# One written order for VectorE and ScalarE from the first product on, and what stands where in it

## The chip, the cores and the metric

The kernel runs on one core of one Trainium2 chip, in one launch. The metric is the device time of that launch in microseconds (us). Engines are named as in the profile: PE is TensorE (matmuls), PEld its weight load, DVE is VectorE, ACT is ScalarE, POOL is GpSimd, SP is SyncE, which here only issues DMAs.

## The reference, cut to what matters

One transformer block on 512 tokens of width 1024, in float32. `x` is normalised and multiplied by one wide matrix; the product is split into the inputs of two branches and of their gates.

```python
n = rmsnorm(h, g_mix[l])
proj = n @ w_in[l]
(gq, gk, gv, gr, z_gf, z_gb, cq, ckv, kr, z_ma, z_mb) = jnp.split(proj, SPLIT_IDX, axis=-1)
y_gla = gla_branch(...)   # 4 heads of gated linear attention, both directions
y_mla = mla_branch(...)   # 8 heads of latent attention with rotary positions
merged = jax.nn.sigmoid(z_ma) * y_gla + jax.nn.sigmoid(z_mb) * y_mla
h = h + merged @ w_out[l]
m = rmsnorm(h, g_mlp[l])
h = h + jnp.square(jax.nn.relu(m @ w_ff1[l])) @ w_ff2[l]
return rmsnorm(h, g_final)
```

In the gated linear attention each head has decays: `log_sigmoid(z @ w_gate + b) / 16`, summed up along the tokens, and their exponentials scale `q` and `k`. `gv` and `gr` are 1024 wide each, `gq` and `gk` 128 wide for each of 4 heads, `z_mb` 1024 wide.

## The kernel before, in words

**Split products.** Every float32 operand of a matmul is split into a rounded high part and a low remainder, and each product is three matmuls (`mm3`: high by high, high by low, low by high). The split is one ACT instruction (the high part, a copy) and one DVE instruction (the remainder, a subtraction), lines 93 and 94. So before PE can use a weight, ACT and then DVE must have worked on it. Split weights live in `halves`: four buffers of high and four of low parts, used in turn. A new split has to wait until PE has finished with the buffer it gets.

**The stages.** The first product (`first`, lines 315 to 351) multiplies the normalised input by the weights of `gq` and `gk` of head 0 and of two pieces of `z_mb`. Beside it runs the sum of squares of `x` (`xss`), whose root is spread over partitions (`xdg`, `xrs`, `R`). Then come, on PE: `zb2` and `zb3` (two more pieces of `z_mb`, 24 matmuls each), the seven products of `gr`, the seven products of `gv`, with single products put in between (the "fillers"), and then the four heads (`bd`, `sc`, `gla0o` and so on), the latent attention, the output product `wo` and the feed-forward part `f`, `gx`, `gz`. The change touches what lies between the first product and the first head.

**The seven products.** `gr` and `gv` are each computed as a product of 2 x 2 blocks by seven block products instead of eight (class `Seven`), in the order 1, 2, 5, 6, 3, 7, 4. Each has 24 matmuls of 128 x 512. Sums and differences of the left blocks are made by POOL (`x_sums`: `xy`, `xz`) and split by ACT and DVE (`xsy`, `xsz`; in the changed kernel `xs`). Differences of the right blocks are made by DVE in place (`less`, line 598: tiles `grw`, `gvw`). `prepare(m)` makes the difference, if there is one, and the split of the weights of product m (`gr50h`, `gr50l`, `gr51h`, `gr51l` for product 5: two pieces, high and low); `product(m)` issues its matmuls and what reads the result. Products 1, 6, 7 and 4 add up in one pair of PSUM banks (`grx`, `gvx`), 5 and 3 in a second (`grz`, `gvz`), 2 in a third (`grw`, `gvw` as outputs of PE). After 1, 5 and 6 ACT copies the partial result out (line 645: `gra`, `grc`, `grb`); after 2, 3 and 7 DVE adds the bank to such a copy (line 650), and a "sink" follows: a tanh and a multiplication for `gr` (lines 658 and 659), a split for `gv` (lines 97 and 98). As 4 goes on in the banks of 7, its first matmuls must wait until DVE has read them after 7.

**The fillers.** `zb4` is put behind product 2 of `gr`, the small product `zk` (gate inputs and rotary key, 16 matmuls, weights `wz`) behind product 7 of `gr`, `gq1` behind product 2 of `gv`. `gk1` stands between 7 and 4 of `gv`. From `zk` come `z4` and then the gates of head 0: `gatef`, `gateb` (one matmul each), then `l` (abs, exp, a table load, ln, a table load), scans `rrf`, `rrb`, differences `diff`, `difb`, exponentials `eef`, `eeb`, small ones `e3f`, `e3b` (`gates_begin`, `gates_end`).

**What sets the order.** A scheduler orders the instructions of each engine, except where the kernel pins them: `in_program_order(start, engines)` makes the instructions issued since `start` follow each other as written. Before the change DVE and ACT are pinned in the first product (all engines, from `fixed`) and again from `heads_from` on, which stands just ahead of the gates of head 0; in between, a chain of `goes_behind` only keeps the DVE work of one `prepare` behind that of the one before. PE is pinned from `ordered` on throughout.

## Time and profile before

| what | us |
|---|---|
| median of 3 runs | 785.69 (785.46 to 786.38) |
| the profiled execution, its own time | 784.01 |
| its span, first to last instruction | 782.3 |
| PE busy in the span | 763.6 |
| DVE, ACT, POOL busy | 571.2, 443.8, 113.4 |
| mean granted clock of PE | 0.994 of full speed |

The profile is of one execution. Its span leaves out 1.7 us of that execution's own time, and that time lies 1.7 us below the median of the three runs. Views used are the page (busy times, 40 slices), the chain of waits of an engine, the timeline of an engine (start, duration, the instruction's line and operands; in square brackets the idle time ahead of it and what ended that), and windows (busy time of each engine in a stretch, with PE's granted clock, called PEclk).

### The profile page before, as it was taken

To read this page: it belongs to the slowest core of one execution; us is meant where nothing else is said; L and a number is where in the kernel's file an instruction comes from. 1 tells how busy PE (TensorE), PEld (TensorE's weight loads), DVE (VectorE), ACT (ScalarE), POOL (GpSimd) and SP (SyncE) were. 2 spreads that over 40 slices of the span, in tenths; PEclk is the share of its full clock that TensorE was granted. 3 is DMA by queue.
4 is the path that set the end of the run, shared out by engine and by line. 5 is a ranking of instruction groups with operands and counts; after the bars stand their busy time and mean duration, and the time that the engine had idled before them with its cause. 6 is when DMAs were issued, how large, how long until landed. Compare 5 with 4: busy or idle time off the path is not lost.

```text
span 782.3 us, 10154 instructions
## 1 busy us (share of the span) xinstructions
PE 763.6 (98%) x3768; PEld 642.4 (82%) x3768; DVE 571.2 (73%) x850; ACT 443.8 (57%) x749; POOL 113.4 (14%) x190
## 2 busy tenths in 40 slices
PE   9989999799999999999999999999999999999996
PEld 7768878598888888888888898888888888888885
DVE  7788896666656867699973578874787578848695
ACT  7564657364747556688853366435553455436644
POOL 0710001314426004211120000000000000000014
PEclk9999999899999999999999999999999999999999
DMA  9806110112123524222033731155106511560002
GB/s 324 282 28 181 41 28 27 41 52 72 54 54 82 121 38 103 76 82 68 28 119 97 268 110 54 52 181 145 40 16 202 147 46 35 162 182 8 27 1 107
DMA packets 93185, 73.94 MB, mean 95 GB/s; under 512 B 15088, under 2 KB 74480, under 8 KB 93136
## 3 DMA queue, kind: packets, MB, share of 16 engines
q1 hardware_dynamic: 92048, 70.14, 30.4%
q10 hardware_dynamic: 864, 2.38, 0.9%
q0 software_dynamic: 224, 0.79, 0.3%
q8 instruction: 29, 0.48, 0.3%
q14 instruction: 20, 0.16, 0.1%
HBM read 69.62 MB, written 2.10 MB: 92 GB/s over the span
## 4 chain that ended last, share of the span: by engine, by line
PE 89%; DVE 6%; ACT 2%; issue 1%; DMA 1%; POOL 0%; SPq 0%; POOLq 0%; DVEq 0%
PE f L89 8%; PE f L88 7%; PE f L90 7%; PE gx L88 4%; PE gx L89 4%; PE gx L90 4%; PE first L323 2%; PE za L88 2%; PE za L89 2%; PE wo L90 2%; PE wo L89 2%; PE gz L89 2%; PE za L90 2%; PE gz L88 2%; PE gz L90 2%; PE wo L88 2%
## 5 line engine op out<-in xcount | busy, mean ns | idle before, releaser
L1395 POOL DMA_DIRECT2D gfin<-in_g_final x1 | 0.7, 653 | 282.6 <-PE f L90 282.6
L1220 DVE TENSOR_TENSOR w<-w,w 128x1024 f32<-128x1024 f32 x32 | 38.8, 1223 | 0.4
L892 DVE TENSOR_REDUCE top<-s 128x1 f32<-128x512 f32 x32 | 21.8, 681 | 5.2 <-PE s L90 5.1
L895 ACT ACTIVATE e<-s,top 128x512 f32<-128x512 f32 x32 | 21.9, 687 | 5.6 <-DVE top L892 3.0
L457 POOL COPY v3f<-rrf 128x4 f32<-128x4 f32 x4 | 2.8, 710 | 148.6 <-DVE rrf L446 148.6
L1167 DVE TENSOR_TENSOR h<-gx,h 128x512 f32<-128x512 f32 x32 | 21.6, 687 | 1.8 <-PE gx L90 1.8
L94 DVE TENSOR_TENSOR pT<-tp,pT 128x512 fp32r<-128x512 f32 x32 | 21.6, 679 | 0.8 <-ACT pT L93 0.7
L93 ACT ACTIVATE pT<-tp 128x512 fp32r<-128x512 f32 x32 | 19.0, 596 | 3.9 <-PE tp L909 3.7
L909 PE MATMUL tp<-ident,e 128*128 128x128 f32 x128 | 19.2, 272 | 0.0
L927 POOL TENSOR_TENSOR tb<-tb,za 128x512 f32<-128x512 f32 x8 | 11.2, 1406 | 54.8 <-DVE tb L926 40.4
L88 PE MATMUL av<-pT,v 128*128 128x256 f32 x64 | 19.1, 298 | 0.0
L1273 ACT ACTIVATE fa<-f 128x512 f32<-128x512 f32 x32 | 18.6, 581 | 0.0
L89 PE MATMUL av<-pT,v 128*128 128x256 f32 x64 | 18.5, 288 | 0.0
L909 PEld LDWEIGHTS tp<-ident,e 128*128 128x128 f32 x128 | 15.5, 140 | 3.5 <-PE s L90 0.6
L90 PE MATMUL av<-pT,v 128*128 128x256 f32 x64 | 18.2, 285 | 0.0
L93 ACT ACTIVATE gbh<-y 128x512 fp32r<-128x512 f32 x16 | 10.2, 635 | 14.0 <-DVE y L1290 14.0
L94 DVE TENSOR_TENSOR sc<-sc,sc 128x512 fp32r<-128x512 f32 x16 | 10.9, 691 | 9.5 <-ACT sc L93 9.5
L93 ACT ACTIVATE sc<-sc 128x512 fp32r<-128x512 f32 x16 | 9.3, 597 | 11.5 <-DVE sc L532 11.5
L88 PE MATMUL s<-kbuf,q 96*128 96x512 f32 x32 | 14.0, 438 | 1.2 <-DVE grb L707 0.9
L93 ACT ACTIVATE b_10h<-w 128x1024 fp32r<-128x1024 f32 x7 | 7.4, 1062 | 12.1 <-PE gx L90 6.0
L93 ACT ACTIVATE b_20h<-w 128x1024 fp32r<-128x1024 f32 x7 | 7.4, 1061 | 12.1 <-PE gz L90 6.0
L93 ACT ACTIVATE b_00h<-w 128x1024 fp32r<-128x1024 f32 x7 | 7.4, 1060 | 12.0 <-PE gx L90 6.0
(1569 smaller groups left out, 2890.5 us busy)
## 6 DMA issues: line engine op xcount, KB each, us to landing
w<-in_w_ff SPq DMA_DIRECT2D x64, 256.0 KB, 3.6
grw<-in_w_in SPq DMA_DIRECT2D x8, 512.0 KB, 7.8
gvw<-in_w_in SPq DMA_DIRECT2D x8, 512.0 KB, 4.6
x<-in_xt SPq DMA_DIRECT2D x8, 256.0 KB, 5.4
vw<-in_w_first SPq DMA_DIRECT2D x8, 256.0 KB, 5.3
h<-in_x ACTq DMA_DIRECT2D x4, 512.0 KB, 5.3
out<-ms SPq DMA_DIRECT2D x7, 256.0 KB, 2.2
q<-ro SPq DMA_DIRECT2D x16, 64.0 KB, 2.3
```

What stands on the lines that cost most here:

```text
L88: nc.tensor.matmul(acc, lh, rh, start=start, stop=False, skip_group_check=onto)
L89: nc.tensor.matmul(acc, lh, rl, start=False, stop=False, skip_group_check=onto)
L90: nc.tensor.matmul(acc, ll, rh, start=False, stop=stop, skip_group_check=onto)
L93: nc.scalar.activation(hi, src, AF.Copy)
L94: rest.tensor_tensor(lo, src, raw(hi), op=ALU.subtract)
L323: nc.tensor.matmul(f_accs[i], a[:, i * P : (i + 1) * P], b, start=k == 0 and x == 0, stop=k == KD - 1 and x == 2)
L892: nc.vector.tensor_reduce(top, acc, axis=AX.X, op=ALU.max, negate=True)
L895: nc.scalar.activation(e, acc, AF.Exp, bias=top, accum_out=tot)
L909: nc.tensor.transpose(tp[:, k * P : (k + 1) * P], e[:, k * P : (k + 1) * P], ident)
L1167: nc.vector.tensor_tensor(hc, acc, hc, op=ALU.add)
L1220: nc.vector.tensor_tensor(wq[dst][g], wq[x][g], wq[y][g], op=op)
L1273: nc.scalar.activation(a, acc, AF.Relu)
```

## The change

It does these things:

- DVE and ACT are pinned in program order from the first product (`fixed`) to the end of the loop over the heads, instead of in two separate stretches. What the scheduler had interleaved between them is now done as written; the `goes_behind` of `prepare` goes.
- The weights of `zb2` and `zb3` are loaded and split during the first product (`begin_late`): their high parts on ACT ahead of the eight scalings of `x`, the low part of `zb2` on DVE while POOL takes the root, that of `zb3` behind `xdg`. Their matmuls keep their place, but what reads them (`z`, tanh) comes behind `prepare(1)` and `prepare(2)` of `gr`.
- The splits of the sums `xy` are taken out of `x_sums` and put at product 2 of `gr`, behind the split of `zb4`; all splits of `xz` stand together ahead of `prepare(3)`.
- `zk` moves as a filler from product 7 of `gr` to product 6. At a product with a filler, `prepare` of the one after next now stands between the product and the filler's matmuls; at the others it stands ahead of the product, as before. So at product 7 of `gr`, `prepare(1)` of `gv` now stands ahead of what reads product 7.
- The gates of head 0 begin behind product 5 of `gv` instead of product 6, and end behind product 6; `prepare(7)` stands between. `prepare(4)` and what reads product 3 follow, and `begin_qk(1, 1)`, which splits `gk1`, comes behind them. On PE the two gate matmuls move from behind product 6 to ahead of it. `gk1` keeps its place between 7 and 4 on PE.
- In what follows products 2, 3 and 7, both additions stand ahead of both sinks, instead of addition, sink, addition, sink.

No instruction is added or removed on PE, DVE, ACT or POOL.

```diff
@@ rstd_diag
         nc.gpsimd.tensor_tensor(r, r, mhalf.to_broadcast([P, NT]), op=ALU.pow)
+        if meanwhile:
+            meanwhile()
...
     x_tot = feature_sums(sq, "x")
+    zb_early = [begin_late(C_ZB + f * P, f"zb{f}", tag) for f, tag in ((2, "at"), (3, "mm"))]
+    for k in range(KD):
+        nc.scalar.activation(xraw[k], xraw[k], AF.Copy, scale=gmix[:, k : k + 1])
     first_with(6)
     first_with(7)
-    x_diag = rstd_diag(x_tot, D, "x", False)
+    x_diag = rstd_diag(x_tot, D, "x", False, zb_early[0][1])
+    zb_early[1][1]()
...
@@ x_sums
-            for u, k in ((a, p), (b, p + KD // 2)):
-                nc.scalar.activation(u, u, AF.Copy, scale=gmix[:, k : k + 1])
...
-            sy = u4(f"xsy{p}")
-            split(sy[:, 0], sy[:, 1], y)
...
-    def more_x_sums():
-        for p, z in enumerate(x_z):
...
+    def split_sums(sums, at_lo, at_hi):
+        for p, src in enumerate(sums):
+            hl = u4(f"xs{at_lo}{p}")
+            split(hl[:, 0], hl[:, 1], src)
+            x_left[p][at_lo] = hl[:, 0, LO], hl[:, 1, LO]
+            x_left[p][at_hi] = hl[:, 0, HI], hl[:, 1, HI]
...
@@ Seven.prepare
-            if prepared:
-                goes_behind((at, traced()), prepared[-1], SPLITTERS[1:])
-            prepared.append((at, traced()))
@@ Seven.product
+                cs = {2: self.c11, 3: self.c12, 7: self.c22}[m]
+                for acc, c in zip(accs, cs):
                     nc.vector.tensor_tensor(c, acc, c, op=ALU.add)
+                for rb, c in enumerate(cs):
                     self.sink(rb + (2 if m == 7 else 0), int(m != 2), c, c)
...
-    zb_gate(2, "at")
-    zb_gate(3)
...
-        (0, 7): (lambda: z_chunk_begin("mm"), z_chunk_run),
+        (0, 6): (lambda: z_chunk_begin("mm"), z_chunk_run),
...
-    for a, m in steps[:2]:
-        sevens[a].prepare(m)
-    for n, (a, m) in enumerate(steps[:-3]):
+    sevens[0].prepare(1)
+    finish_zb(2, zb_early[0])
+    sevens[0].prepare(2)
+    finish_zb(3, zb_early[1])
+    for n, (a, m) in enumerate(steps[:-4]):
...
+            if n == 1:
+                split_sums(x_y, 5, 6)
             sevens[a].product(m)
+            sevens[ahead[0]].prepare(ahead[1])
             rest(w)
+            continue
         if n == 2:
-            more_x_sums()
+            split_sums(x_z, 7, 3)
         sevens[ahead[0]].prepare(ahead[1])
...
-        if not filled:
-            sevens[a].product(m)
+        sevens[a].product(m)
...
-    heads_from = traced()
     gated_now = gates_begin(0)
+    sevens[1].prepare(7)
+    sevens[1].product(6)
+    parts = gates_end(gated_now)
     sevens[1].prepare(4)
+    sevens[1].product(3)
     w_k = begin_qk(1, 1)
-    parts = gates_end(gated_now)
-    sevens[1].product(3)
     sevens[1].product(7)
...
-    in_program_order(heads_from, SPLITTERS)
+    in_program_order(fixed, SPLITTERS)
     in_program_order(ordered, PE_ONLY)
```

More of the change, by code (lines that the diff above doesn't have):

```diff
@@ L231, in proj_begin, with begin_late @@
         return wh, wl, ps(tag, name)
-    def begin_late(col, name):
+    def begin_late(col, name, tag="mm"):
         wf = stage(KD, P, name)
@@ L241, in lows @@
             nc.vector.tensor_tensor(wl, wf, raw(wh), op=ALU.subtract)
-        return (wh, wl, ps("mm", name)), lows
+        return (wh, wl, ps(tag, name)), lows
     def proj_run(begun, src, half=None, ks=range(KD)):
@@ L268, in feature_sums, with rstd_diag @@
         return tot
-    def rstd_diag(tot, n, name, scaled):
+    def rstd_diag(tot, n, name, scaled, meanwhile=None):
         r = r_x if name == "x" else sm(f"{name}r")
@@ L371, in qk_normed @@
         return n
+    zb_early = [begun for begun, _ in zb_early]
     qk = {(0, x): qk_normed(0, x, f_accs[x]) for x in range(2)}
@@ L543, in tile_block @@
     x_left = []
-    prepared = []
     x_y = []
@@ L550, in x_sums @@
         add = nc.gpsimd.tensor_tensor
-        for p in range(KD // 2):
-            a, b = xraw[p], xraw[p + KD // 2]
-            for u, k in ((a, p), (b, p + KD // 2)):
-                nc.scalar.activation(u, u, AF.Copy, scale=gmix[:, k : k + 1])
+        half = KD // 2
+        for p in range(half):
+            a, b = xraw[p], xraw[p + half]
             y = u2(f"xy{p}")
@@ L557, in x_sums @@
             add(y[:, HI], y[:, LO], a[:, LO], op=ALU.subtract)
-            sy = u4(f"xsy{p}")
-            split(sy[:, 0], sy[:, 1], y)
             x_y.append(y)
-            upper, lower = xT[p], xT[p + KD // 2]
+            upper, lower = xT[p], xT[p + half]
             x_left.append({m: (src[:, 0, c], src[:, 1, c]) for m, src, c in (
-                (1, upper, LO), (2, lower, LO), (4, lower, HI), (5, sy, LO), (6, sy, HI),
+                (1, upper, LO), (2, lower, LO), (4, lower, HI),
             )})
-        for p in range(KD // 2):
-            a, b = xraw[p], xraw[p + KD // 2]
+        for p in range(half):
+            a, b = xraw[p], xraw[p + half]
             z = u2(f"xz{p}")
@@ L572, in tile_block @@
     x_z = []
-    def more_x_sums():
-        for p, z in enumerate(x_z):
-            sz = u4(f"xsz{p}")
-            split(sz[:, 0], sz[:, 1], z)
-            x_left[p][7] = sz[:, 0, LO], sz[:, 1, LO]
-            x_left[p][3] = sz[:, 0, HI], sz[:, 1, HI]
+    def split_sums(sums, at_lo, at_hi):
[4 more added lines that the diff above has]
+            x_left[p][at_hi] = hl[:, 0, HI], hl[:, 1, HI]
     class Seven:
@@ L604, in prepare @@
             x = {1: 0, 2: 2, 5: 0, 6: 0, 3: 3, 7: 1, 4: 2}[m]
-            at = traced()
             if m == 5:
@@ L641, in product @@
                         begin and p == 0, p == KD // 2 - 1, not begin)
-            for rb, acc in enumerate(accs):
-                if m in (1, 5, 6):
-                    c = {1: self.c11, 5: self.c22, 6: self.c12}[m][rb]
+            if m in (1, 5, 6):
+                for acc, c in zip(accs, {1: self.c11, 5: self.c22, 6: self.c12}[m]):
                     nc.scalar.activation(c, acc, AF.Copy)
-                elif m == 4:
+            elif m == 4:
+                for rb, acc in enumerate(accs):
                     self.sink(2 + rb, 0, acc, u2(f"{self.name}d"))
-                else:
-                    c = {2: self.c11, 3: self.c12, 7: self.c22}[m][rb]
+            else:
+                cs = {2: self.c11, 3: self.c12, 7: self.c22}[m]
+                for acc, c in zip(accs, cs):
                     nc.vector.tensor_tensor(c, acc, c, op=ALU.add)
+                for rb, c in enumerate(cs):
                     self.sink(rb + (2 if m == 7 else 0), int(m != 2), c, c)
@@ L930, in tile_block @@
     y1 = []
-    def zb_gate(f, tag="mm"):
-        g2.append(gated(proj_T(C_ZB + f * P, f"zb{f}", tag), f"b{f}")[1])
     summed = traced()
     x_sums()
-    zb_gate(2, "at")
-    zb_gate(3)
     sevens = [Seven(C_GR, "gr", gr_rows), Seven(C_GV, "gv", gv_rows)]
@@ L967, in tile_block @@
     ordered = traced()
-    for a, m in steps[:2]:
-        sevens[a].prepare(m)
-    for n, (a, m) in enumerate(steps[:-3]):
+    sevens[0].prepare(1)
[3 more added lines that the diff above has]
+    for n, (a, m) in enumerate(steps[:-4]):
         ahead = steps[n + 2]
-        filled = (a, m) in fillers
         if a == 0:
@@ L975, in tile_block @@
                 sevens[1].load(x)
-        if filled:
+        if (a, m) in fillers:
             first_part, rest = fillers[a, m]
```

## The prediction

> **What bounds the kernel.** I read the page first, then PE's chain of waits, then PE's granted clock by stretches, then the timelines of PE, DVE and ACT between 20 and 160 us.

> ```profile
> span 782.3 us, 10154 instructions
> PE 763.6 (98%) x3768; PEld 642.4 (82%) x3768; DVE 571.2 (73%) x850; ACT 443.8 (57%) x749; POOL 113.4 (14%) x190
> ...
> PE gvx L88 <- DVE gvc L650: 4.4, 2, 3.7
> PE grx L88 <- ACT gr10h L93: 1.3, 1, 1.3
> PE zb L90 <- DVE zb4l L94: 1.1, 1, 1.1
> PE gq L90 <- DVE gq1l L94: 1.0, 1, 1.0
> PE grx L89 <- DVE gr10l L94: 0.8, 1, 0.8
> PE zb L90 <- DVE zb2l L94: 0.6, 1, 0.6
> ...
> 130.00:141.00 11.00, 7.59 (x34) 5.96 (x32) 8.67 (x17) 5.67 (x10) 3.54 (x16) 1.00 0.17 48
> 141.00:150.00 9.00, 8.01 (x22) 5.87 (x23) 7.22 (x10) 2.40 (x3) 2.96 (x3) 0.62 0.23 61
> ```

> PE is busy for 98% of the span. No instruction comes or goes, so time can only be won or lost where PE waits, or where its clock (the first figure behind the engines in a windows row) is low. All six waits shown lie in the stretch that the change reorders. The longest, 3.7 us ahead of product 4 of `gv`, has a stretch at 0.62 of full clock behind it.

> **Measure.** PE's ideal pace comes from two starts with 48 matmuls between them:

> ```profile
> 109.78 0.39 PE L88 MATMUL gvz<-gv50h,xsy 128*128 128x512 f32 x1
> 120.66 0.39 PE L427 MATMUL gatef<-z,gate_f 128*128 128x512 f32 x1
> ...
> 52.09 1.22 DVE L94 TENSOR_TENSOR gr51l<-grw,gr51h 128x1024 fp32r<-128x1024 f32 x1
> 53.22 1.22 DVE L598 TENSOR_TENSOR grw<-grw,grw 128x1024 f32<-128x1024 f32 x1
> 54.35 0.69 DVE L650 TENSOR_TENSOR gra<-grw,gra 128x512 f32<-128x512 f32 x1
> 54.95 1.22 DVE L94 TENSOR_TENSOR zb4l<-zb4f,zb4h 128x1024 fp32r<-128x1024 f32 x1
> ...
> 49.86 1.05 ACT L93 ACTIVATE gr50h<-grw 128x1024 fp32r<-128x1024 f32 x1
> 50.81 1.05 ACT L93 ACTIVATE gr51h<-grw 128x1024 fp32r<-128x1024 f32 x1
> 51.76 1.66 ACT L93 ACTIVATE xsz<-xz 128x512 fp32r<-128x512 f32 x3
> 55.52 0.71 ACT L658 ACTIVATE tr<-gra,r_half 128x512 f32<-128x512 f32 x1
> ```

> 10.88 us over 48 is 0.2267 each, 5.44 for a product. From start to start DVE needs 1.13 us for 1024 columns (53.22 less 52.09) and 0.60 for 512; ACT 0.95 (50.81 less 49.86), 0.52 for 512 (1.66 over three, less the tail), 0.6 where it reads PSUM. I follow each queue of the changed kernel in its new order with these figures; a matmul's result is there 0.39 after its start. These sums are estimates, each good to some 0.4 us.

> **Waits that go, 22 to 61 us.**

> ```profile
> 28.77 0.40 PE L88 MATMUL zb<-xT,zb2h 128*128 128x512 f32 x1
> 48.64 0.39 PE L88 MATMUL grw<-gr20h,xT 128*128 128x512 f32 x1
> 61.36 0.39 PE L88 MATMUL grz<-gr50h,xsy 128*128 128x512 f32 x1
> ```

> From `zb2` to product 2 of `gr` PE spends 19.87 us on 72 matmuls worth 16.32: 3.55 lost. From there to product 5, 12.72 on 48 worth 10.88: 1.84 lost. Afterwards `zb2l` is made beside the root, at 23 to 25 us, `gr10h` no longer stands behind what reads `zb2` and is ready by about 35, `gr10l` by 36, and PE wants them at 39.65. POOL's sums run beside these DVE instructions and may slow them; the cover is over 3 us. `zb4h` starts when the first half of product 2 frees its buffer (48.0), `zb4l` ends at 50.3; it is wanted at 51.0. So 5.4 us go, and product 5 starts at 55.97.

> **New wait 1, `zk`.** It is wanted behind product 6, at 66.85, instead of behind product 7. DVE's queue up to its weights, from `zb4l` at 49.1: nine instructions of 1024 columns (`zb4l`, four differences, `gr60l`, `gr61l`, `gr30l`, `gr31l`), 10.2; eight splits of `xs`, two additions, two multiplications, `zb4`'s reader and `wz`, 14 of 512, 8.4; waits for tanh, `gr60h` and the chain tanh of `zb4`, first split of `xz`, about 1.7. That ends at 69.5: PE waits 2.7 us. The queue hangs on PE's own product 2, so it moves with PE.

> **New wait 2, product 4 of `gr`.** It adds onto the banks of product 7 and waits for DVE's additions. `zk` covered that:

> ```profile
> 83.12 3.79 PE L404 MATMUL zk<-xT,wzh 128*128 128x512 f32 x16
> ```

> Now `gv10l` and `gv11l` stand ahead of these additions on DVE, and `gv11h` must wait for the buffer that product 7's last matmul frees. So behind product 7's end (84.2): 0.16 for the last result, 1.05 `gv11h`, 1.13 `gv11l`, 0.69 the addition, handovers of 0.1: 3.1 us, with 3.0 of PE idle. The second addition hides behind the first three matmuls.

> **`gq1`.** Before:

> ```profile
> 103.07 0.39 PE L88 MATMUL gq<-xT,gq1h 128*128 128x512 f32 x1
> ```

> To `gv50h` at 109.78 this is 6.71 for 24 matmuls worth 5.44: 1.27 lost. Afterwards `gq1l` ends at about 104.4, wanted at 104.1: 0.4 is left, 0.8 saved. To here: -5.4 + 2.7 + 3.1 - 0.8 = -0.4; with the roundings kept and 0.1 for the slow first matmul behind each wait, -0.3, and `gk1` is wanted at 131.7.

> **New wait 3, `gk1`, for the one at product 4 of `gv`.**

> ```profile
> 131.99 0.39 PE L88 MATMUL gk<-xT,gk1h 128*128 128x512 f32 x1
> 137.20 0.39 PE L90 MATMUL gk<-xT,gk1l 128*128 128x512 f32 x1
> 141.30 0.61 PE L88 MATMUL gvx<-gv40h,xT 128*128 128x512 f32 x1 [3.71 <-DVE gvc L650]
> 150.64 0.39 PE L88 MATMUL zb<-xT,zb5h 128*128 128x512 f32 x1
> ...
> 122.36 0.68 ACT L428 ACTIVATE l<-gatef,gvec 128x512 f32<-128x512 f32 x1
> 126.03 1.06 ACT L433 ACTIVATE l<-l 128x1024 f32<-128x1024 f32 x1
> ...
> 131.71 1.37 DVE L446 TENSOR_TENSOR_SCAN rrf<-mf,l 128x128 f32<-128x128 f32 x4
> 133.11 0.69 DVE L450 TENSOR_TENSOR diff<-rrf 128x512 f32<-128x512 f32 x1
> 135.12 0.69 DVE L450 TENSOR_TENSOR difb<-rrb 128x512 f32<-128x512 f32 x1
> ...
> 140.56 0.69 DVE L650 TENSOR_TENSOR gvc<-gvx,gvc 128x512 f32<-128x512 f32 x1
> 142.71 0.68 DVE L650 TENSOR_TENSOR gvc<-gvx,gvc 128x512 f32<-128x512 f32 x1
> ```

> Before, PE ran through `gk1`, then waited for `gvc` behind scans and sinks: 18.65 us from `gk1` to `zb5` for 10.88 of matmuls. The new order takes the 2.15 between the two `gvc` additions away and moves the gates forward, so this wait goes. But `gk1h` now stands on ACT behind the whole gate chain and product 3's sink. Counted from product 5's end (115.0): `gv31h` and two copies to 117.3; the gates from abs to ln take 4.7 (122.36 to the end at 127.09 before), to 121.9; `gv70h`, `gv71h`, `gv70l`, `gv71l` to 125.2; scans and differences 4.1 (131.7 before to 135.8), to 129.3; `eeb` and `e3b` 1.3, to 130.6; `gv40h`, `gv41h`, `gv40l`, `gv41l`, additions and two splits of `gv` to 135.8; `gk1h` to 136.85, `gk1l` to 138.1. PE is ready at 131.7: it waits 5.15 us for the high part and 0.85 for the low one, and idles 5.0 at a stretch. `zb5` starts at 148.6, 16.9 behind `gk1`: 1.75 less. Sum without any change of clock: -0.3 - 1.75 = -2.1 us. ACT's table load lies inside the wait for `diff`. SP's reordered loads (`gk1f`, two of `gvw`, `zb5f`) land over 10 us ahead of use.

> **The clock.** Product 4 of `gv` took 9.34 us from 141.30 to 150.64, 3.9 over its 5.44; three matmuls at half clock take 1.36, and the second `gvc` addition ended 2.09 behind the start, so 0.7 of it is the second wait and about 3.2 the price of half clock. And at the end of the kernel:

> ```profile
> 775.42 0.28 PE L90 MATMUL gend<-b_31h,ga 128*128 128x256 f32 x1
> ...
> 779.00:780.00 1.00, 0.00 (x0) 0.00 (x0) 0.00 (x0) 0.00 (x0) 0.00 (x0) 0.92 0.91 330
> 780.00:782.30 2.30, 0.00 (x0) 0.00 (x0) 0.00 (x0) 0.00 (x0) 0.00 (x0) 0.50 0.29 109
> ...
> 42.02 0.51 PE L88 MATMUL grx<-gr10h,xT 128*128 128x512 f32 x1 [1.33 <-ACT gr10h L93]
> ```

> There the clock fell at 779.84 (0.92 over the slice), 4.1 us behind the last matmul; at `gvx`, where the matmul ahead ended at 137.59, it had fallen by the matmul of 141.30 (0.61 long instead of 0.39), after some 3.7 to 4; behind the idle 1.33 it did not fall. So I take half clock only where PE idles longer than about 3.8: at `gk1`, not at 2.5 and 3.0, which are nearer to it than to 1.33 but below both falls. Bounds for each of these two: 0 and 3.2. At `gk1` part of the slow time lies under the wait for `gk1l`: 2.5, between 0 and 3.2. [...]

> Forecast: -2.1 + 2.5 = +0.4 us on the profiled execution's 784.01 (span 782.3 to 782.7), and as much on the median 785.69: 786.1. What follows `zb5` keeps its order on every engine and shifts along.

> **Rivals.** [...] 0.25. Second, slower: the clock halves behind the 2.5 and 3.0 too. It decides if a stretch mostly idle is enough, somewhere between 1.33 and 3.7; for it: at `gvx` the clock stayed at half for 6.8 us (0.62 over 9) though PE was at work for most of them, so a stretch need not be wholly idle. One of them gives 786.1 + 3.2 = 789.3, both 792.5. 0.28. Third: my queues are too slow by over a microsecond in each wait, since several of DVE's small waits overlap; then about 5 us less and no half clock, 781. 0.05. That the order stays as the scheduler had it is out: the built kernel's instructions stand in the order told here. 0.02 for other cancellations. My forecast: 0.40.

> **Chances.** A difference of 0.2% (1.6 us) is about what a measurement can tell. Faster: most of the first rival, the third, a little of the forecast, 0.25. Slower: nearly all of the second and the forecast where waits come out 1.2 us longer, 0.40. Same: the rest, 0.35. Range: from just under the first rival, 783.2, to the second with one fall and longer waits, 790.8. The likeliest case alone would be 784.8 to 787.4.

> **What would show it.** In the profile after: no wait at `zb2`, `grx`, `zb4`; PE waits for DVE at `zk` (2.7), at `grx` of product 4 (3.1, `grc`), for ACT `gk1h` (5.0) and `gk1l`; none at `gvx`. PEclk under 1 only from about 137 to 143. I am wrong if `zk` or product 4 starts without a wait, or if slow matmuls follow them.

## The result and the profile after

| kernel | median, us | lowest to highest | runs |
|---|---|---|---|
| before | 785.36 | 783.81 to 786.54 | 20 |
| changed | 786.75 | 785.11 to 789.31 | 20 |

The ratio of changed to before is 1.0018, with a 95% interval of 1.001 to 1.0026: 1.4 us slower, just under the 0.2% that the prediction named as the bound. 786.1 was forecast. The profiled execution of the changed kernel is the longest of its twenty: 789.31 us, span 787.6, mean granted clock 0.988. How its own time relates to the median turns out to be the main question below.

The page and PE's chain of waits, after (the waits' columns: us in total, times, longest us):

```profile
span 787.6 us, 10144 instructions
PE 766.8 (97%) x3768; PEld 645.9 (82%) x3768; DVE 569.7 (72%) x850; ACT 442.1 (56%) x749; POOL 113.2 (14%) x190
...
PE gk L88 <- ACT gk1h L93: 4.9, 1, 4.9
PE grx L88 <- DVE grc L650: 3.1, 1, 3.1
PE zk L411 <- DVE wzh L94: 2.8, 1, 2.8
...
PE gq L90 <- DVE gq1l L94: 0.4, 1, 0.4
```

The waits at `zb2`, at product 1 of `gr`, at `zb4` and ahead of product 4 of `gv` are gone. Three others stand in their place, where the prediction put them and with the releasers that it named. PE is busy for 3.2 us more than before although it has the same 3768 matmuls: some of them ran slower. PE's timeline shows which:

```profile
29.51 0.39 PE L88 MATMUL zb<-xT,zb2h 128*128 128x512 f32 x1
56.71 0.39 PE L88 MATMUL grz<-gr50h,xs 128*128 128x512 f32 x1
70.50 5.54 PE L411 MATMUL zk<-xT,wzh 128*128 128x512 f32 x16 [2.76 <-DVE wzh L94]
90.07 0.77 PE L88 MATMUL grx<-gr40h,xT 128*128 128x512 f32 x1 [3.15 <-DVE grc L650]
98.31 0.39 PE L88 MATMUL gvx<-gv10h,xT 128*128 128x512 f32 x1
...
142.61 0.80 PE L88 MATMUL gk<-xT,gk1h 128*128 128x512 f32 x1 [4.88 <-ACT gk1h L93]
150.47 0.39 PE L88 MATMUL gvx<-gv40h,xT 128*128 128x512 f32 x1
155.91 0.39 PE L88 MATMUL zb<-xT,zb5h 128*128 128x512 f32 x1
```

From `zb2` to product 5 there are 120 matmuls in 27.20 us, 0.2267 each: the front of the stretch runs without a gap, where before it took 32.59. Then each wait is followed by slow matmuls. `zk` takes 5.54 instead of 3.79 (1.75 more), product 4 of `gr` 8.24 instead of 5.44 (2.80 more), `gk1` 7.86 instead of 5.44 (2.42 more, a small wait for its low part included). The windows show the granted clock (the first figure behind the engines) and where its edges lie:

```profile
68.50:72.00 3.50, 1.50 (x6) 1.24 (x7) 3.50 (x5) 0.51 (x2) 0.00 (x0) 0.99 0.71 265
72.00:75.30 3.30, 3.30 (x9) 2.60 (x8) 1.95 (x2) 0.74 (x1) 0.00 (x0) 0.50 0.72 210
85.60:89.00 3.40, 1.32 (x6) 0.75 (x4) 3.14 (x4) 2.35 (x3) 0.00 (x0) 1.00 1.06 373
89.00:95.80 6.80, 5.73 (x14) 4.52 (x15) 2.83 (x5) 1.52 (x3) 0.00 (x0) 0.50 0.11 26
...
136.80:140.20 3.40, 0.93 (x5) 0.43 (x3) 2.92 (x4) 1.39 (x2) 0.15 (x2) 1.00 0.01 2
140.20:147.00 6.80, 4.35 (x9) 3.01 (x10) 6.13 (x10) 4.56 (x6) 0.00 (x0) 0.50 0.25 72
147.00:150.00 3.00, 3.00 (x14) 2.46 (x13) 3.00 (x4) 0.00 (x0) 1.32 (x2) 0.99 0.23 49
```

The clock is at one half from 72.0 to 75.3, from 89.0 to 95.8 and from 140.2 to 147.0: one, two and two stretches of 3.4 us. Their starts lie 17.0 and 51.2 us apart, 5 and 15 times 3.4. Ahead of each stands a stretch of 3.4 to 3.5 in which PE worked for 1.50, 1.32 and 0.93 us: under half of the time, but it was not idle throughout.

One stretch of 3.4 us at half clock lowers the mean clock of the whole by 1.7/785, 0.0022, and costs up to 1.7 us, an estimate from the lengths and the 0.50 in the windows above. The twenty runs list mean clocks between 0.994 (three runs, 785.1 to 785.3 us) and 0.988 (two runs, 788.8 and 789.3); eight lie at 0.990 (786.9 to 787.5). With no such stretch in the middle the clock is 0.998 (the kernel with filled waits, below), so these runs have, by this estimate, two to five of them, the median run three to four.

### The profile page after: what moved, and what is told of

It is laid out like the page before. It is cut to its first block, busy times and chain, and to the rows that moved or that the text cites. A ratio compares the mean times of both kernels' runs of the same rounds, so it can differ in the third digit from the quotient of the medians.

```text
span 787.6 us, 10144 instructions
## 1 busy us (share of the span) xinstructions
PE 766.8 (97%) x3768; PEld 645.9 (82%) x3768; DVE 569.7 (72%) x850; ACT 442.1 (56%) x749; POOL 113.2 (14%) x190
## 3 DMA queue, kind: packets, MB, share of 16 engines
q1 hardware_dynamic: 92048, 70.14, 30.2%
## 4 chain that ended last, share of the span: by engine, by line
PE 88%; DVE 6%; ACT 5%; issue 1%; POOL 0%; POOLq 0%; ACTq 0%; DVEq 0%
PE f L89 7%; PE f L88 7%; PE f L90 7%; PE gx L88 4%; PE gx L89 4%; PE gx L90 4%; PE first L325 3%; PE za L88 2%; PE wo L89 2%; PE za L89 2%; PE za L90 2%; PE wo L88 2%; PE gz L88 2%; PE gz L89 2%; PE wo L90 2%; PE gz L90 2%
## 5 line engine op out<-in xcount | busy, mean ns | idle before, releaser
L94 DVE TENSOR_TENSOR pT<-tp,pT 128x512 fp32r<-128x512 f32 x32 | 21.6, 679 | 0.8 <-ACT pT L93 0.7
L93 ACT ACTIVATE pT<-tp 128x512 fp32r<-128x512 f32 x32 | 19.0, 594 | 4.0 <-PE tp L910 3.8
L88 PE MATMUL av<-pT,v 128*128 128x256 f32 x64 | 19.1, 298 | 0.0
L89 PE MATMUL av<-pT,v 128*128 128x256 f32 x64 | 18.5, 289 | 0.0
L90 PE MATMUL av<-pT,v 128*128 128x256 f32 x64 | 18.2, 285 | 0.0
L93 ACT ACTIVATE gbh<-y 128x512 fp32r<-128x512 f32 x16 | 10.1, 633 | 14.0 <-DVE y L1291 14.0
L94 DVE TENSOR_TENSOR sc<-sc,sc 128x512 fp32r<-128x512 f32 x16 | 10.9, 690 | 9.5 <-ACT sc L93 9.5
L93 ACT ACTIVATE sc<-sc 128x512 fp32r<-128x512 f32 x16 | 9.3, 595 | 11.5 <-DVE sc L539 11.5
L88 PE MATMUL s<-kbuf,q 96*128 96x512 f32 x32 | 14.0, 437 | 1.2 <-DVE grb L708 0.9
L93 ACT ACTIVATE b_20h<-w 128x1024 fp32r<-128x1024 f32 x7 | 7.4, 1059 | 12.1 <-PE gz L90 6.0
L93 ACT ACTIVATE b_10h<-w 128x1024 fp32r<-128x1024 f32 x7 | 7.4, 1059 | 12.1 <-PE gx L90 6.0
L93 ACT ACTIVATE b_00h<-w 128x1024 fp32r<-128x1024 f32 x7 | 7.4, 1058 | 12.1 <-PE gz L90 6.0
```

The costliest lines, as they stand in the source:

```text
L88: nc.tensor.matmul(acc, lh, rh, start=start, stop=False, skip_group_check=onto)
L89: nc.tensor.matmul(acc, lh, rl, start=False, stop=False, skip_group_check=onto)
L90: nc.tensor.matmul(acc, ll, rh, start=False, stop=stop, skip_group_check=onto)
L93: nc.scalar.activation(hi, src, AF.Copy)
L94: rest.tensor_tensor(lo, src, raw(hi), op=ALU.subtract)
```

## The experiments

Each kernel was timed beside runs of the kernel before on the same chip; three groups of four, in which before had medians of 785.5, 785.8 and 785.3, so a difference between kernels of different groups, or to the changed kernel's 786.75 (before: 785.4 there), is uncertain by some 0.4 us beyond its own spread. Two of the theories named in the expectations are A, the three waits cost their idle time and mostly half a clock behind each, and B, the prediction's own: half clock only at `gk1`. C says that DVE is full there and any wait taken away comes back.

| run | median, us | ratio to before (95%) | clock of most runs |
|---|---|---|---|
| 1 `zk` weights early | 784.84 | 0.9993 (0.9984 to 1.0002) | 0.990 |
| 2 additions of product 7 first | 783.57 | 0.9974 (0.9964 to 0.9984) | 0.992 to 0.994 |
| 3 `gk1` split early | 780.14 | 0.9930 (0.9918 to 0.9943) | 0.994 |
| 4 three waits filled | 782.67 | 0.9967 (0.9955 to 0.9980) | 0.998 |
| 5 `zb2`, `zb3` weights late | 795.77 | 1.0125 (1.0110 to 1.0140) | 0.986 |
| 6 `zk` behind product 7 | 780.48 | 0.9941 (0.9929 to 0.9954) | 0.994 |
| 7 runs 3 and 6 together | 774.26 | 0.9857 (0.9842 to 0.9873) | 0.996 to 0.999 |
| 8 sinks between the additions | 794.22 | 1.0111 (1.0098 to 1.0124) | 0.986 |
| 9 run 7 and three small moves | 772.60 | 0.9844 (0.9830 to 0.9858) | 0.998 |
| 10 idle of 2.1 and 2.0 left | 784.98 | 0.9997 (0.9987 to 1.0006) | 0.993 to 0.997 |
| 11 idle of 1.2 and 1.1 left | 782.80 | 0.9973 (0.9962 to 0.9984) | 0.998 |
| 12 before, its wait filled | 783.43 | 0.9979 (0.9970 to 0.9987) | 0.995 |

### What the clock costs: the waits filled

`busy(bank, n)` issues n matmuls of 128x512 whose results are overwritten; the remarks behind the calls are added here.

```diff
+        busy(acc, 11)                   # ahead of zk, into its own bank
...
+            if m == 4 and self.name == "gr":
+                busy(self.zs[0], 12)    # ahead of product 4 of gr
...
+    busy(w_k[2], 20)                    # ahead of gk1
```

> The three waits stay, but PE is given matmuls to do in them whose results are overwritten: 11 of 128x512 ahead of zk (2.5 us of the 2.76), 12 ahead of product 4 of gr (2.7 of 3.15), 20 ahead of gk1 (4.5 of 4.88). Nothing on DVE or ACT is changed. Theory A: every start after a wait is as late as before, the half clock behind them is gone: 783.0 us (782.2 to 783.8), granted clock 0.995 or more, and zk 3.8 long instead of 5.5. Theory B: only gk1's 1.6 to 2.5 go, 784.2 to 785.2. If the clock has no part in it: 786.7.

Measured: 782.67, 4.1 below the changed kernel, at a clock of 0.998. PE's timeline and windows of this kernel:

```profile
67.59 2.65 PE L409 MATMUL zk<-xT 128*128 128x512 f32 x11
70.51 3.93 PE L416 MATMUL zk<-xT,wzh 128*128 128x512 f32 x16 [0.26 <-DVE wzh L94]
...
80.00:100.00 20.00, 19.56 (x87) 15.93 (x86) 15.59 (x19) 10.10 (x13) 0.00 (x0) 1.00 0.29 84
130.00:150.00 20.00, 19.13 (x83) 15.20 (x83) 14.55 (x18) 8.12 (x12) 7.82 (x20) 1.00 0.20 54
```

`zk` starts at 70.51 as before (70.50 in the profile above), so the wait is as long, but it takes 3.93 us and not 5.54, and the clock is full throughout. Work that is thrown away made the kernel faster than both originals. So the changed kernel pays some 4.1 us for its clock, more than B's 2.5 at `gk1` alone allowed (784.2 to 785.2).

### How much idle time it takes

> The changed kernel with its waits partly filled: 3 matmuls of 128x512 at zk and 5 at product 4 of gr, which leaves 2.1 and 2.0 us of idle, and 21 at gk1, which leaves about 0.1. The filled kernel took 782.7 at a mean clock of 0.998. Theory A (a wait of about 2 us is enough where most of it falls into one stretch of 3.4 us): some of the runs fall, one halved stretch costing up to 1.7 us: runs between 782.6 and 786, median 783.5 to 785, clock 0.993 to 0.998. If an idle of 2.0 is never enough: 782.7, clock 0.998 in all runs.

> As the run before, with 7 and 9 matmuls, which leaves 1.2 and 1.1 us of idle at zk and at product 4, 0.1 at gk1. Below half of 3.4 us no single stretch is mostly idle: 782.7, clock 0.998 in all runs. If any idle of over a microsecond can halve the clock: 783.5 to 785 with some runs below 0.996.

The edits are the same three lines with 3, 5, 21 and with 7, 9, 21 matmuls. Measured: 784.98 (twelve runs from 782.63 to 785.79, clocks from 0.999 to 0.993) and 782.80 (six runs from 782.67 to 783.21, all at 0.998 or above). `zk` in the first and in the second kernel:

```profile
69.43 5.52 PE L416 MATMUL zk<-xT,wzh 128*128 128x512 f32 x16 [2.07 <-DVE wzh L94]
```

```profile
69.67 3.94 PE L416 MATMUL zk<-xT,wzh 128*128 128x512 f32 x16 [1.17 <-DVE wzh L94]
```

2.07 us of idle time can halve the clock (0.70 over 69.50 to 75.20 in the first profile), 1.17 did not in any of six runs (0.998 or above). Between the two kernels PE starts `zk` only 0.24 us apart, but the median differs by 2.2. In the first one the mean clock changes from run to run, 0.993 to 0.999, by the estimate above from no slow stretch to two or three. That it depends on how much of the wait falls into one stretch of 3.4 us, as A has it here, was not shown.

A single wait of 2 us is not needed. In the profile of run 6 (below) the clock fell at `gq1`, behind two waits of 1.30 and 0.52 us that lie in one stretch:

```profile
98.25:101.66 3.41, 1.58 (x7) 0.69 (x5) 2.73 (x4) 2.02 (x4) 0.00 (x0) 1.00 0.00 0
101.66:105.08 3.42, 3.42 (x8) 2.69 (x9) 3.23 (x5) 1.33 (x2) 0.00 (x0) 0.50 0.53 153
```

Nor do the profiles give an exact limit. In run 1 a stretch with PE at work for 1.50 us passed, and the next one stayed at full clock:

```profile
130.73:134.14 3.41, 1.50 (x7) 0.93 (x5) 2.37 (x3) 1.96 (x3) 0.57 (x4) 1.00 0.01 2
134.14:137.55 3.41, 0.45 (x2) 0.30 (x2) 3.07 (x5) 2.28 (x3) 0.00 (x0) 1.00 0.00 0
```

### Each wait taken away

The first run puts the split of the `zk` weights ahead of `prepare(3)`:

```diff
-        (0, 6): (lambda: z_chunk_begin("mm"), z_chunk_run),
+        (0, 6): (lambda: z_early, z_chunk_run),
...
             split_sums(x_z, 7, 3)
...
+            z_early = z_chunk_begin("mm")
...
         sevens[ahead[0]].prepare(ahead[1])
```

> The split of the zk weights is put ahead of the right-hand differences of product 3 of gr on ACT and DVE, so PE should not wait at zk (2.8 us in the profile of the changed kernel); nothing else is moved. Theory A, the three new waits cost their idle time and mostly half a clock behind each: 2.8 of idle and up to 1.75 of slow zk matmuls go, PE waits at product 4 of gr and at gk1 stay at about 3.1 and 4.9, 783.0 us (782.0 to 784.2). Theory B, half clock only behind gk1: 2.8 go and no more, 784.0. Theory C, DVE is the bound from 50 to 140 us, so a wait that is taken away comes back at a later product: 786.0 to 787.0, with a longer wait at product 3 or 7 of gr or at gq1.

```profile
PE grx L88 <- DVE grc L650: 4.5, 1, 4.5
```

784.84, above A's range. The wait at `zk` is gone, but the one at product 4 of `gr` has grown from 3.1 to 4.5. In this profile DVE goes from `wz` at 64.19 to the additions at 84.87 with only short gaps: half of C is right here, the queue itself is what PE waits for.

The second run puts product 7's additions ahead of `gv`'s first split:

```diff
+        if (a, m) == (0, 7):
+            sevens[a].product(m)
         sevens[ahead[0]].prepare(ahead[1])
...
-        sevens[a].product(m)
+        if (a, m) != (0, 7):
+            sevens[a].product(m)
```

> At product 7 of gr what reads its banks stands ahead of the split of gv's product 1 on DVE and ACT. The wait ahead of product 4 of gr falls from 3.1 to about 0.9 (the last result 0.16, one addition 0.69), the other two waits stay. Theory A: 2.2 of idle go, and the slow stretch behind it (product 4 took 8.2 us instead of 5.44 in the profile) goes where a run had it: 783.2 (782.0 to 784.5). Theory B: 784.5, and no slow matmuls to lose. Theory C: the 2.2 come back in gv, at product 1 or 2 or at gq1: 786.0 to 787.0.

```profile
PE zk L411 <- DVE wzh L94: 2.8, 1, 2.8
...
PE grx L88 <- DVE grc L650: 0.5, 1, 0.5
```

783.57, as A expected: 3.2 less than the changed kernel for 2.6 us of idle time, and nothing came back in `gv`.

The third run splits `gk1` around the gates:

```diff
     sevens[1].product(6)
+    w_k, lows = begin_late(C_GK + P, "gk1")
     parts = gates_end(gated_now)
+    lows()
...
     sevens[1].product(3)
-    w_k = begin_qk(1, 1)
```

> gk1's weights are split earlier: the high part on ACT behind product 6's copies and ahead of the table load and the exponentials, the low part on DVE behind the differences, where DVE stood idle for 2.3 us. Theory A: the waits of 4.9 and 0.85 at gk1 go, with about 1.6 of slow matmuls behind them, and gvx waits under 0.5: 779.5 (778.5 to 781.0). Theory B gives nearly the same here, 779 to 780, since it has the half clock at this place. Theory C: DVE was late with the additions of gvc too, so the wait goes to product 4 of gv as it was before the change (3.7): 783.0 to 785.0.

```profile
PE grx L88 <- DVE grc L650: 3.1, 1, 3.1
PE zk L411 <- DVE wzh L94: 2.8, 1, 2.8
...
PE gvx L88 <- DVE gvc L650: 0.3, 1, 0.3
```

780.14, 6.6 below the changed kernel. The old wait at product 4 of `gv` (3.7) does not return: 0.3 is left. The place of one split of two instructions is worth 0.8% of the kernel.

### zk put back, and both orders together

> zk goes back behind product 7 of gr, with the split of its weights ahead of that for product 4, and product 7's additions ahead of gv's first split; gk1 is left as changed. Theory A: the waits at zk (2.8) and at product 4 (3.1) both go with the slow stretches behind them, a wait of about 0.8 at product 3 takes their place (its low part is made at 68.7 and wanted at 68.0): 786.75 - 5.1 - 2.5 = 779.2 (778.2 to 780.5). Theory C: DVE's queue, full from 64 to 87 us in the run with zk's weights early, makes PE wait elsewhere for 2 us or more, at product 3, 7 or zk: 781.5 to 783.5.

```diff
-        (0, 6): (lambda: z_chunk_begin("mm"), z_chunk_run),
+        (0, 7): (lambda: z_early, z_chunk_run),
...
+        if n == 4:
...
+            z_early = z_chunk_begin("mm")
...
         sevens[ahead[0]].prepare(ahead[1])
```

> zk behind product 7 as in the run before this one, and gk1 split early as in the third experiment. If the three waits and their slow stretches add up (theory A): 780.1 from the run with gk1 early, less 2.8 + 3.1 - 0.8 of idle and about 2.5 of half clock: 772.5 (771.3 to 774.0), granted clock 0.998, no wait of PE over 1 us between 20 and 160 us but for what is left at product 3. Theory C: 775 to 778.

Measured: 780.48 and 774.26. Run 7's waits:

```profile
PE gq L88 <- ACT gq1h L93: 1.3, 1, 1.3
...
PE grz L89 <- DVE gr30l L94: 0.8, 1, 0.8
PE gq L90 <- DVE gq1l L94: 0.5, 1, 0.5
PE gvx L88 <- DVE gvc L650: 0.3, 1, 0.3
```

Both came out 1.3 to 1.8 above the expected value, run 7 also 0.3 above A's range: with PE earlier, `gq1`'s split is late by 1.8 us, where 0.4 was counted on. Two of run 7's four runs (775.2 and 775.8) show a clock of 0.996 where its profile has 0.999; that they paid for a slow stretch behind these two waits at `gq`, as run 6's profile did, is likely but not shown. Apart from that the savings of runs 3 and 6 add up (6.6 and 6.3 below the changed kernel singly, 12.5 together).

> The run with both orders (774.3), and three small moves for the PE waits that its profile still shows: gq1's split goes ahead of that for product 5 of gv (waits of 1.3 and 0.5 at gq), the reader of zb4 goes behind the split for product 3 of gr (0.8 at its first low part), the split of the gate weights goes ahead of product 4 of gr. Theory A (waits and the half clock behind them are all that this stretch costs): 1.8 + 0.7 of idle go, and in those runs that had it a half-clock stretch: 771.2 (770.3 to 772.5). Theory C (DVE full from 94 to 103 us): the wait at gq goes to product 5 of gv, 773 to 774.5.

```diff
+            if (a, m) == (0, 7):
+                split_gates()
             rest(w)
...
+        if n == 7:
+            gq_early = begin_qk(1, 0)
         sevens[ahead[0]].prepare(ahead[1])
+        if n == 2:
+            g2.append(gated(zb4[2], "b4")[1])
...
```

772.60, 1.6% under the kernel before and the lowest median of all, 0.1 above A's range. The waits at `gq` are gone; the second move failed. PE's wait, and the ACT timeline that explains it:

```profile
PE grz L88 <- ACT grc L643: 1.9, 1, 1.9
...
67.88 0.63 ACT L368 ACTIVATE tb<-zb 128x512 f32<-128x512 f32 x1 [4.86 <-DVE zb L366]
68.42 1.07 ACT L643 ACTIVATE grc<-grz 128x512 f32<-128x512 f32 x2
```

The tanh of `zb4` now waits on ACT for a DVE instruction far back in its queue, and the copies that free the banks for product 3 stand behind it: 1.9 us in place of 0.8.

### Two parts of the change undone

> The fixed order stays, but the weights of zb2 and zb3 are loaded and split behind the first product, where the kernel before had them; on DVE that is behind the four readers of the first product, which wait for R (about 30.3 us). The low part of zb2 should then be there at about 33.8 instead of 24, and PE, which wants it at 30.2, waits 3.6 us; what follows is late by the same, with a chance of half clock behind it. Theory A (the early splits are what gains the time at the front, and the new waits hang on PE's own progress): 786.75 + 3.6 + 0 to 1.7, 790.3 to 792.2. Theory C (DVE bounds the stretch from 50 us on, so a later start of PE shortens the wait at zk): 787.5 to 789.5, with a wait at zk under 1.5 us.

```diff
-    zb_early = [begin_late(C_ZB + f * P, f"zb{f}", tag) for f, tag in ((2, "at"), (3, "mm"))]
...
+    zb_early = [proj_begin(w_in, C_ZB + f * P, f"zb{f}", tag) for f, tag in ((2, "at"), (3, "mm"))]
     sevens = [Seven(C_GR, "gr", gr_rows), Seven(C_GV, "gv", gv_rows)]
```

```profile
PE gk L88 <- ACT gk1h L93: 4.9, 1, 4.9
PE zb L88 <- ACT zb2h L93: 4.8, 1, 4.8
PE grx L88 <- DVE grc L647: 3.1, 1, 3.1
PE zk L408 <- DVE wzh L94: 2.8, 1, 2.8
```

795.77, 3.6 above the range: the wait is 4.8, since the high part stands behind two tanhs on ACT, which was overlooked, and the clock falls behind it too (0.91 over 20 to 40 us), as it does behind the other three waits (0.986 over the whole). The lengths of these three have not changed by 0.1 although PE comes to them over 5 us later. They hang on PE's own products, as the prediction had it; C's shorter wait at `zk` is refuted. This is not what the early place is worth against the kernel before: there, with the order left to the scheduler, ACT made `zb2h` at 23.55, and PE waited 0.6 at `zb2`. It is what the late place costs once the order is pinned.

> The changed kernel with the additions behind products 2, 3 and 7 as before: addition, sink, addition, sink. At product 4 of gr the second bank is then read 1.5 us later (tanh, a handover and a multiplication stand between), and the three matmuls of the first bank cover 0.7 of it: PE waits 0.8 to 1.4 more there, 787.9 (787.2 to 788.6). At gv the second addition is over long before product 4, behind gk1, so nothing is lost there. If the order of additions and sinks is worth nothing: 786.7.

```diff
                 for acc, c in zip(accs, cs):
                     nc.vector.tensor_tensor(c, acc, c, op=ALU.add)
-                for rb, c in enumerate(cs):
+                    rb = 0 if c is cs[0] else 1
                     self.sink(rb + (2 if m == 7 else 0), int(m != 2), c, c)
```

```profile
PE gk L88 <- ACT gk1h L93: 6.4, 1, 6.4
PE grx L88 <- DVE grc L650: 4.9, 2, 4.6
PE zk L411 <- DVE wzh L94: 4.2, 1, 4.2
```

794.22, 6.3 above the expected value. All three waits grow by 1.4 to 1.8 us. DVE behind product 2 of `gr`, in this kernel and then in the changed one:

```profile
52.46 0.69 DVE L650 TENSOR_TENSOR gra<-grw,gra 128x512 f32<-128x512 f32 x1
53.94 0.69 DVE L660 SCALAR_TENSOR_TENSOR gra<-tr,gra 128x512 f32<-128x512 f32 x1 [0.79 <-ACT tr L659]
54.55 0.68 DVE L650 TENSOR_TENSOR gra<-grw,gra 128x512 f32<-128x512 f32 x1
56.03 0.69 DVE L660 SCALAR_TENSOR_TENSOR gra<-tr,gra 128x512 f32<-128x512 f32 x1 [0.79 <-ACT tr L659]
```

```profile
53.44 1.28 DVE L650 TENSOR_TENSOR gra<-grw,gra 128x512 f32<-128x512 f32 x2
54.92 1.31 DVE L660 SCALAR_TENSOR_TENSOR gra<-tr,gra 128x512 f32<-128x512 f32 x2 [0.20 <-ACT tr L659]
```

With the order pinned, each sink makes DVE stand still for 0.79 us until ACT answers, twice per product; with both additions first it is 0.20 once, as the second addition covers the answer to the first. That is 1.4 us for each product, and the clock falls further (0.986). The expectation looked only at which bank is read when, and missed that everything behind in DVE's queue is late by as much.

### The kernel before, filled

> The kernel before the change with 15 matmuls put into its wait ahead of product 4 of gv (3.4 of the 3.7 us; results overwritten). Nothing else is changed. By the prediction's price of half clock there, 3.2 us: 782.3 (781.6 to 783.2), clock 0.998. That is the changed kernel with its waits filled (782.7) or a little below it; then the change without the clock is worth nothing to -1 us. If before paid nothing for its clock: 785.4, and the change without the clock gains 2.7.

```diff
     finish_qk(1, 1, w_k)
+    for _ in range(15):
+        nc.tensor.matmul(w_b[2], xT[0][:, 0, 0:P], xT[0][:, 0, :], start=True, stop=True)
     sevens[1].product(4)
```

783.43, 1.8 below before and just above the range. Eleven of twelve runs are at 0.995 to 0.996 (783.0 to 784.1), one at 0.998: 781.59. So before paid for its clock too. Most runs keep a slow stretch somewhere even now; where is open, as the profiled execution is the one that has none.

The price of half clock at product 4 of `gv` was less than the prediction's 3.2. In this run's profile, at full clock, the product takes 7.03 us (141.19 to 148.22) where it took 9.34: 2.3. The second wait, which the prediction took as 0.7 beside the slow matmuls, is longer without them:

```profile
143.33 0.50 PE L88 MATMUL gvx<-gv40h,xT 128*128 128x512 f32 x1 [1.18 <-DVE gvc L650]
```

At full clock on both sides the change does not pay: 782.67 with its waits filled against 781.59, though the latter is a single run. By the medians (783.43) it gains 0.8, since most runs of the filled kernel before keep a slow stretch.

## Why the prediction was right, and where it was not

**Waits that go: right.** 5.4 us was the sum; 32.59 less 27.20 is 5.39. In this execution `zb2` starts 0.74 later than in that of before, and product 5 another 27.20 behind it; without the 0.74 that is 55.97, the predicted value. (The start of `zb2` lies between 28.4 and 29.5 in the profiles of the other eleven kernels that do not wait there, before's own filled version among them, so the 0.74 is no effect of the order.) Beside POOL's sums the splits were slower, and the cover held: in the changed kernel's profile `gr11l` took 1.75 us on DVE and `gr20l` 1.53, `gr21l` behind the sums 1.21, and PE waited for none of them.

**Lengths of the new waits: right.** 2.7, 3.0 and 5.0 of idle time were forecast, 2.76, 3.15 and 4.88 came; 0.4 at `gq1`, 0.4 came. No wait at product 4 of `gv`, as said. Without the 0.74 and without the slow matmuls (1.75, 2.80 and 2.42 less the 0.85 counted for the low part of `gk1`, 6.1 together) the profiled 789.31 would be 782.5; the sum without any change of clock was 781.9.

**The clock: wrong.** The step that failed is "So I take half clock only where PE idles longer than about 3.8". The two falls seen in the trace of before showed that 3.7 is enough; that less is not enough was read into them. Idle times of 2.76, 3.15 and, in run 10, 2.07 did it. The term was 2.5 at `gk1` alone; the filled kernel measured 4.1 for all three. It is what the prediction had named as a sign of being wrong: slow matmuls follow the waits at `zk` and product 4. And 3.4 us without a matmul were not needed: the stretches ahead of the three falls had PE at work for 0.93 to 1.50 us. The same holds for the fall at `gvx` in the trace of before:

```profile
141.30:143.00 1.70, 1.46 (x3) 0.64 (x3) 0.96 (x2) 0.71 (x1) 0.00 (x0) 0.57 0.00 0
```

A mean of 0.57 over these 1.70 us means half clock for 1.46 of them, so the clock fell some 0.24 us after PE was back at work at 141.30, and the 3.4 us ahead of the fall were not wholly idle.

**Why the number still held.** By two errors that partly cancel, so by luck: the filled kernel lies 2.7 below before's 785.36 (the forecast without new clock cost was -2.1), and 4.1 comes on top, 1.4 in all; +0.4 was forecast. The 2.7 is not all the order's doing. The sum was taken from a profile with a clock of 0.994, but of the 56 runs of before beside the experiments 47 show 0.992, by the 0.0022 for each about one slow stretch more, of which the prediction knew nothing. The other nine lie at 783.5 to 783.8, and the profiled execution at 784.0; below these the filled kernel is by 0.8 to 1.3 only.

**The rivals.** The second one, half clock behind the shorter waits too, is the mechanism that runs 4 and 10 show, yet its price of 3.2 at each was too high (1.75 and 2.80 in the longest of twenty runs, less in most by their clocks; 2.3 in before itself, run 12); that is why the median lies at 786.75 and not at 789.3 or 792.5. The first rival, no fall anywhere and 783.6, on which the low end of the range stands, would need a clock of 0.998; no run of the changed kernel shows it, the highest clock was 0.994 and the lowest time 785.11. The third is refuted by the measured lengths.

**What the prediction did not see** is that large parts of the change cancel: the fixed order without its three waits, and with run 9's small moves, is worth 12.7 us (772.60 against 785.26), and the additions ahead of the sinks alone 7.5 us in the changed kernel (794.22 against 786.75), its slow stretches included. The prediction's queues have both additions first, but it gave that a price only in `gv`'s 2.15. What it is worth in run 9's kernel was not measured.

## What to carry to other kernels

When an order is pinned by hand, look for every instruction that waits for another engine's answer, and put independent work behind the question: in run 8 the 1.4 us lost there for each product were lost for the whole queue, and PE paid 1.4 to 1.8 us at each of three later waits. Price a wait of TensorE not by its length alone: here waits of 2.02 and 2.07 us (run 10), or two shorter ones close together (1.30 and 0.52, run 6), could cost a slow stretch more, and a few matmuls of throw-away work in the gaps showed at once how much of the time was clock (4.1 us, run 4). Before a change is dropped because it nets out at nothing, take its new waits one at a time; here one split moved by a few lines was worth 6.6 us.
